# A written order for the late columns of a hybrid decoder layer, keys turned 256 rows at a time, and RWKV's propagators in one stretch

## The chip, the cores and the metric

The kernel runs on one core of a Trainium2 chip. The metric is the device time of one execution in microseconds; lower is better. The engines named below are PE (TensorE, matrix products and transposes), DVE (VectorE), ACT (ScalarE), POOL (GpSimd) and SP (SyncE, whose queue issues most DMAs).

## The reference

One inference step of one layer, for a prompt of 1024 tokens and eight decode samples. Everything reads the same normalised input `h`:

```python
h = rms_norm(x, ln_g)
q, kv, gates, z_nsa, u, z_rw, q_mem, z_mem = split_in(h @ w_in)
o_nsa = ...   # 8 heads: compressed blocks, top-16 selected blocks and a window of 512, mixed by gates
# RWKV-7, 4 heads of 64, per token:
sa = einsum('bhvk,bhk->bhv', s, -kk_t)
s  = s * w_t + sa * b_t + v_t * k_t
y_t = einsum('bhvk,bhk->bhv', s, r_t)
# memory: 256 rows
mkv = rms_norm(mem, g) @ w_kv        # keys get their own norm
o_mem = softmax(norm(q_mem) @ k.T * SCALE) @ v
cat = concat([o_nsa * silu(z_nsa), norm(y) * silu(z_rw), o_mem * silu(z_mem)])
y = x + cat @ w_out
```

The compressed keys come from an MLP over 32 rows at stride 16 (`compress`). The outputs also hold the new key and value rows, the final RWKV state and the memory's keys and values.

## The kernel before

All is 32-bit. A product of full precision is made of three fast ones: each operand is split into a high part (ACT copies it to the fast format, `whi`) and a low part (DVE subtracts, `wlo`), and high times high, high times low and low times high are summed in PSUM.

The work has three phases. In phase 1 the input projection is done in 21 *columns*, blocks of 128 output columns of `w_in`, in the order of the table `ORDER`. A column is done for two halves of the tokens. Its products are named `p_pr`, 24 per 512 tokens: 24 of 512 columns in one half, and 24 of 256 with 24 of 264 in the other, where the last 8 are the samples. Its result is drained by ACT and DVE (`zt` for the gate columns, `nr_o` and the like for queries and keys) and stored by SP to a scratch in memory (`z_d`, `q_d`, `k_d`, `v_d`).

The recurrence of RWKV is done in four quarters Q of the tokens in the matrix form of the delta rule (`rwkv_prep`, `rwkv_state`). It is a chain of small products on PE with evacuations on DVE and ACT between them, so `drive` puts column products between its steps as fill: a step yields the microseconds of PE work that should stand behind it. The order on PE is there written by the code: `InOrder` ties every PE instruction to the one before it, and keeps a running sum of PE time, `clock`. At the end of a quarter, `rwkv_state` forms `p_x` (the corrected rows, drained to `W` by ACT and `UV` by DVE), the propagators `p_g` (drained to `PT` and `GT`), the rows `p_yy`, and four rounds of `p_z<-Zn,PT`, each drained to `Zn`. `rwkv_out` normalises the result and stores it (`y_d<-y_c`). `rwkv_close` turns the final state with two transposes, also named `p_s`, as are the scores of the attention later.

When the fill is used up (17 columns, `EARLY`), the tail of Q = 3 and what follows are on a plain PE: the scheduler of the framework chooses the order by its own costs and priorities. There `ahead` interleaves, eight instructions to one step (`BG`):

- the last four columns (17 to 20), by `self.columns(cols[EARLY:])`, drawn in groups of 8;
- `attn_keys`, eight tiles of 128 key rows: each is loaded twice (two DMAs in 256 B pieces, so that each head stands on both halves of the partitions, `kd`), turned by four transposes (`p_k`) and split into `kh` and `kl`;
- `prompt_cmp` (the compressed keys: turned rows `p_xt`, the products `p_hid`, then `p_co`, whose normalised result is turned by a last `p_k` and drained to `ckh`, `ckl`);
- `mem_kv` (the memory's rows `mx` turned by `p_mT`, split into `mhi` and `mlo`, and 48 products `p_mo` in blocks of two of the eight k tiles), and `q_stack(7)` (the first queries, `p_q`).

Phase 2 is the attention, and begins with the scores `p_s<-kh,qs`; phase 3 is the output projection. PSUM tiles that are used for turning come from one pool of two buffers (tag `tr`); `p_g`, `p_yy`, `p_z` and `p_mo` use another (tag `w`).

```python
            for _ in group(late, 8):
                for _ in islice(bg, BG):
                    pass
```

Of the kernel before, what the change touches and what calls it, by code (L numbers as in the profile page):

```python
# [10 lines left out]
F32 = mybir.dt.float32  # L11
# [15 lines left out]
KB = 2  # L27
FREE = 0
ORDER = [4, 1, 11, 2, 3, 6, 5, 7, 13, 17, 10, 15, 0, 9, 8, 14, 12, 18, 16, 19, 20]
EARLY = 17  # L30
BG = 8
# [82 lines left out]
class Step:  # L114
# [356 lines left out]
    def phase1(self):  # L471
# [8 lines left out]
        with ExitStack() as ctx:  # L480
# [91 lines left out]
            self.pe = nc.tensor  # L572
# [10 lines left out]
            for _ in bg:  # L583
                pass

    def ahead(self):

        def keys():
            for i in range(8):
                self.attn_keys(i)  # L590
                yield
            yield from self.q_stack(7)

        self.mem_x()
        yield from weave(chain(self.prompt_cmp(), self.mem_kv()), keys())
# [232 lines left out]
    def rwkv_state(self, Q):  # L828
# [103 lines left out]
        GT, PT = [None] * 2, [None] * 2  # L932
        half = [slice(p * 64, p * 64 + 64) for p in range(2)]
        for t in range(2):
            GT[t] = self.rs.tile([128, 2, 2, 64], F32, name="GT", tag=f"GT{t}")
            PT[t] = self.rs.tile([128, 2, 2, 64], F32, name="PT", tag=f"PT{t}")
            pgs = [self.pw.tile([128, 4, 64], F32, name="p_g", tag="w") for _ in range(2)]
            for k in range(2):
                for c in range(2):
                    for h in range(2):  # L940
                        for pg, o, p in zip(pgs, half, range(2)):
                            x = AM[o, 2 * p + t, 2 * c + h, 64:128] if k else bkT[t][o, c, p, h * 64:h * 64 + 64]
                            PE.matmul(pg[half[h], 2 * k + c, :], W[t][o, 2 * c + h, :], x, start=True, stop=True)
            for p, pg in enumerate(pgs):
                V.tensor_tensor(PT[t][:, :, p, :], pg[:, 0:2], bc(self.eye2[:, None, :], [128, 2, 64]), op=OP.add)
            for p, pg in enumerate(pgs):
                V.tensor_tensor(GT[t][:, :, p, :], pg[:, 2:4], ar[:, :, t, 1, p, :], op=OP.add)
            if t == 0:
                yield 0.9
# [6 lines left out]
        yield 0.9  # L956
# [8 lines left out]
        for n in range(4):  # L965
            Zn = self.rc.tile([128, 2, 64], F32, name="Zn", tag="Z", bufs=5)
            for c in range(2):
                for h in range(2):
                    PE.matmul(pz[half[h], n, c, :], PT[n // 2][half[h], c, n % 2, :], Zs[n][half[h], c, :],
                              start=False, stop=True, skip_group_check=True)  # L970
            V.tensor_tensor(Zn[:], pz[:, n], bc(self.gC[:, :, n:n + 1], [128, 2, 64]), op=OP.mult)
            Zs.append(Zn)
            if n < 3:
                yield 0.8
        self.Z = Zs[4]
        for t in range(2):
            for c in range(2):
                for p, h in ((0, 0), (1, 1), (1, 0), (0, 1)):
                    PE.matmul(pyy[h][half[1 - p], t, c, :], GT[t][half[h], c, p, :], Zs[2 * t + p][half[h], c, :],
                              start=False, stop=(c == 1), skip_group_check=True)  # L980
# [32 lines left out]
    def rwkv_close(self):  # L1013
        nc, O = self.nc, self.O
        ps = self.pw.tile([128, 2, 128], F32, name="p_s", tag="w")
        for c in range(2):
            nc.tensor.transpose(ps[:64, c, :], self.Z[:, c, :], self.ident[:])
# [15 lines left out]
    def cmp_consts(self):  # L1033

        nc, I = self.nc, self.I
        V, PE = nc.vector, nc.tensor
# [45 lines left out]
    def compress(self, xt, n, hid):  # L1082

        nc = self.nc
        V, A, PE = nc.vector, nc.scalar, self.te
        V.memset(hid[:, :, 63:64], 0.0)
        for e in range(2):
            ps = self.pM.tile([128, n, 64], F32, name="p_hid", tag="m")
            for m in range(8):
                PE.matmul(ps[:], self.w1s[e][:, m].rearrange("p a b -> p (a b)"), xt(e, m), start=(m == 0), stop=(m == 7))  # L1090
            hs = self.wk.tile([64, n, 63], F32, name="c_hs", tag="c_hs", bufs=2)
            A.activation(hs[:], ps[64:, :, 1:], AF.Copy)
            V.tensor_tensor(hs[:], hs[:], ps[:64, :, :63], op=OP.add)
# [4 lines left out]
            yield  # L1098

    def cmp_out(self, hid2):  # L1100
# [3 lines left out]
        nc.tensor.matmul(ps[:, :128], hid2, self.w2d[:].rearrange("p a b -> p (a b)"), start=True, stop=True)  # L1104
# [20 lines left out]
    def mem_kv(self):  # L1125
        nc, I, O = self.nc, self.I, self.O
        V, A, PE = nc.vector, nc.scalar, nc.tensor
        xs = self.mem_rows
        his = [self.slot(j, [128, 4, 256], F32R, f"mhi{j}") for j in (4, 0)]
        los = [self.slot(j, [128, 4, 256], F32R, f"mlo{j}") for j in (5, 1)]  # L1130
        for k in range(8):
            ps = self.pM.tile([128, 512], F32, name="p_mT", tag="m")
            for t in range(2):
                PE.transpose(ps[:, t * 128:(t + 1) * 128], xs[t][:, k * 128:(k + 1) * 128], self.ident[:])
            g = self.v("mem_norm_g", k)
            hi, lo = his[k // 4][:, k % 4, :], los[k // 4][:, k % 4, :]
            A.activation(hi, ps[:, :256], AF.Copy, scale=g)
            V.scalar_tensor_tensor(lo, ps[:, :256], g, hi.bitcast(F32), op0=OP.mult, op1=OP.subtract)
            yield
        po = [self.pw.tile([128, 512], F32, name="p_mo", tag="w") for t in range(2)]  # L1140
        for k in range(0, 8, 2):
            raw = self.wr.tile([128, 2, 512], F32, name="wraw")
            nc.sync.dma_start(raw[:], I["w_mem_kv"][0, k * 128:(k + 2) * 128, :].rearrange("(k p) c -> p k c", p=128))
            wh = self.wp.tile([128, 2, 512], F32R, name="whi")
            wl = self.wp.tile([128, 2, 512], F32R, name="wlo")
            A.activation(wh[:], raw[:], AF.Copy)
            V.tensor_tensor(wl[:], raw[:], wh[:].bitcast(F32), op=OP.subtract)
            yield
            for j in range(2):
                for t in range(2):  # L1150
                    cs = slice(t * 128, (t + 1) * 128)
                    h, l = his[k // 4][:, (k + j) % 4, cs], los[k // 4][:, (k + j) % 4, cs]
                    for i, (a, w) in enumerate(((h, wh), (h, wl), (l, wh))):
                        PE.matmul(po[t][:], a, w[:, j], start=(k + j == 0 and i == 0), stop=(k + j == 7 and i == 2))
            yield
        dst = O["mem_kv_prompt"]
        for t in range(2):
# [5 lines left out]
            yield  # L1163
# [67 lines left out]
    def attn_keys(self, i, tag="m"):  # L1231
        nc = self.nc
        A, G = nc.scalar, nc.gpsimd
        kk = self.kt.tile([128, 4, 2, 64], F32, name="kd4", tag="kd4", bufs=KB)
        for s in range(2):
            nc.sync.dma_start(kk[:, :, s, :], self.k_d[i * 128:(i + 1) * 128, :].rearrange("t (j d) -> t j d", d=64))
        if i % 4 == 0:
            nc.sync.dma_start(self.vs[i // 4][:].rearrange("p k b g d -> p k (b g d)"),
                              self.v_d[i * 128:(i + 4) * 128, :].rearrange("(k p) c -> p k c", p=128))
        ps = self.pM.tile([128, 4, 128], F32, name="p_k4", tag=tag)  # L1240
        for j in range(4):
            nc.tensor.transpose(ps[:, j, :], kk[:, j].rearrange("p s d -> p (s d)"), self.ident[:])
        kh, kl = (x[i // 4][:, :, i % 4 * 128:i % 4 * 128 + 128] for x in (self.kh, self.kl))
        A.activation(kh, ps[:], AF.Copy)
        nc.vector.tensor_tensor(kl, ps[:], kh.bitcast(F32), op=OP.subtract)

    def prompt_cmp(self):
        nc, I, O = self.nc, self.I, self.O
        V, A, G, PE = nc.vector, nc.scalar, nc.gpsimd, nc.tensor
# [11 lines left out]
        for e in range(2):  # L1261
# [4 lines left out]
            xs.append(x)  # L1266
        yield from self.cmp_consts()
# [15 lines left out]
        yield  # L1283
# [1232 lines left out]
```

## Time and profile before

| | us |
|---|---|
| median of three runs | 937.47 (934.78 to 939.75) |
| profiled execution | 936.7, of which the span 934.9 |
| PE busy | 899.3 (96%) |
| DVE, ACT, POOL busy | 648.0, 434.2, 178.7 |
| granted clock of PE, mean | 0.998 |

The span runs from the first to the last instruction that the profile shows. The stretch of the change is the last quarter's tail (from 409 us on), the late columns (to 497 us), and, for the propagators, a few microseconds in each of the three quarters before. A row of a timeline gives the start, the length, the engine, the line of the code, the operation and its tiles, the shape, the number of instructions and, in brackets, the idle time ahead with what ended it. The ends of products on PE are modelled, so the time from one start to the next tells better how fast they follow each other.

### The profile page before, as it was taken

To read this page: it belongs to the slowest core of one execution; us is meant where nothing else is said; L and a number is where in the kernel's file an instruction comes from. 1 tells how busy PE (TensorE), PEld (TensorE's weight loads), DVE (VectorE), ACT (ScalarE), POOL (GpSimd) and SP (SyncE) were. 2 spreads that over 40 slices of the span, in tenths; PEclk is the share of its full clock that TensorE was granted. 3 is DMA by queue.
4 is the path that set the end of the run, shared out by engine and by line. 5 is a ranking of instruction groups with operands and counts; after the bars stand their busy time and mean duration, and the time that the engine had idled before them with its cause. 6 is when DMAs were issued, how large, how long until landed. Compare 5 with 4: busy or idle time off the path is not lost.

```text
span 934.9 us, 24813 instructions
## 1 busy us (share of the span) xinstructions
PE 899.3 (96%) x9911; PEld 762.7 (82%) x9911; DVE 648.0 (69%) x2013; ACT 434.2 (46%) x987; POOL 178.7 (19%) x270
## 2 busy tenths in 40 slices
PE   8999999999999999999899999999999999999998
PEld 7998888877878788778777788888887887887976
DVE  7668679864777559946457866765678996548454
ACT  7654324232443234213446666666566766424211
POOL 2000000000000000000104444544344765112010
PEclk9999999999999999999999999999999999999999
DMA  8521313241321205524429313432130036986561
GB/s 278 130 78 35 104 41 105 61 115 48 84 86 52 77 19 143 136 65 132 138 85 275 99 56 108 132 108 60 32 87 10 10 113 168 330 249 218 179 239 47
DMA packets 134698, 105.96 MB, mean 113 GB/s; under 512 B 34641, under 2 KB 120600, under 8 KB 134456
## 3 DMA queue, kind: packets, MB, share of 16 engines
q1 hardware_dynamic: 129592, 92.64, 33.8%
q0 software_dynamic: 3200, 10.49, 3.2%
q8 instruction: 78, 1.28, 0.5%
q10 hardware_dynamic: 1792, 1.26, 0.5%
q14 instruction: 36, 0.29, 0.1%
HBM read 85.77 MB, written 22.78 MB: 116 GB/s over the span
## 4 chain that ended last, share of the span: by engine, by line
PE 73%; DVE 17%; ACT 5%; DMA 2%; issue 2%; POOL 0%; SPq 0%; DVEq 0%; ACTq 0%
PE p_pr L86 20%; PE p_out L86 9%; PE p_pr L306 5%; PE p_o L86 5%; PE p_s L86 5%; PE p_pT L86 5%; PE p_hid L86 3%; ACT p L1416 2%; DVE p L1409 2%; PE p_it L86 1%; PE p_iy L86 1%; PE p_sc L86 1%; DVE pt L1377 1%; DVE wlo L283 1%; PE p_tk L86 1%
## 5 line engine op out<-in xcount | busy, mean ns | idle before, releaser
L86 PE MATMUL p_pr<-h,whi 128*128 128x512 f32 (+2 forms) x976 | 237.0, 336 | 2.0 <-DVE zt L318 2.0
L86 PEld LDWEIGHTS p_pr<-h,whi 128*128 128x128 f32 x976 | 158.6, 189 | 19.5 <-issue 2.4
L86 PE MATMUL p_pr<-h,wlo 128*128 128x512 f32 (+2 forms) x488 | 157.6, 326 | 0.6 <-DVE wlo L283 0.6
L1447 POOL TENSOR_SCALAR p<-p,fac,gates 128x640 f32<-128x640 f32 (+7 forms) x128 | 103.3, 817 | 110.9 <-DVE fac L1443 71.1
L1416 ACT ACTIVATE p<-p,nm 128x640 f32<-128x640 f32 (+7 forms) x128 | 93.1, 728 | 56.3 <-DVE nm L1409 51.3
L86 PEld LDWEIGHTS p_pr<-h,wlo 128*128 128x128 f32 x488 | 91.4, 189 | 9.3 <-DVE wlo L283 0.8
L86 PE MATMUL p_pT<-ident,p 128*128 128x128 f32 x528 | 70.8, 279 | 6.9 <-POOL p L1447 1.9
L1075 POOL MEMSET w2d<- 128x128 f32 x1 | 0.2, 204 | 377.2 <-PE p_iy L86 377.2
L86 PEld LDWEIGHTS p_pT<-ident,p 128*128 128x128 f32 x528 | 56.8, 140 | 18.1 <-issue 6.6
L1409 DVE CUSTOM_DVE_ANT_0 p<-p_s,bmask 128x512 f32<-128x512 f32 (+7 forms) x96 | 60.3, 659 | 16.1 <-PE p_s L86 15.4
L306 PE MATMUL p_pr<-h,whi 128*128 128x264 f32 (+2 forms) x320 | 69.3, 310 | 0.0
L86 PE MATMUL p_o<-pt,vs 128*64 128x128 f32 x1056 | 67.9, 276 | 0.4 <-DVE cat L1485 0.4
L283 DVE TENSOR_TENSOR wlo<-wraw,whi 128x1024 fp32r<-128x1024 f32 x33 | 40.3, 1221 | 36.9 <-ACT whi L282 32.6
L86 PE MATMUL p_s<-kh,qs 128*128 128x512 f32 (+3 forms) x191 | 65.2, 354 | 0.2 <-DVE nm L1409 0.2
L282 ACT ACTIVATE whi<-wraw 128x1024 fp32r<-128x1024 f32 x34 | 36.0, 1059 | 59.6 <-PE p_pr L86 47.1
L86 PEld LDWEIGHTS p_o<-pt,vs 128*64 128x64 f32 x1056 | 57.0, 137 | 7.5 <-issue 3.9
L86 PE MATMUL p_s<-kl,qs 128*128 128x512 f32 (+3 forms) x192 | 60.3, 334 | 0.0
L1377 DVE COPY pt<-p_pT 128x512 f32<-128x512 f32 (+1 forms) x72 | 48.2, 673 | 13.2 <-PE p_pT L86 12.4
L306 PEld LDWEIGHTS p_pr<-h,whi 128*128 128x128 f32 x320 | 51.5, 188 | 3.1 <-issue 0.2
L86 PE MATMUL p_out<-woh,chi 128*128 128x512 f32 x128 | 51.7, 404 | 0.0
L86 PE MATMUL p_out<-woh,clo 128*128 128x512 f32 x128 | 50.2, 392 | 0.4 <-DVE clo L2352 0.4
L86 PE MATMUL p_out<-wol,chi 128*128 128x512 f32 x128 | 49.9, 390 | 0.0
(551 smaller groups left out, 1884.3 us busy)
## 6 DMA issues: line engine op xcount, KB each, us to landing
wraw<-in_w_in_dram SPq DMA_DIRECT2D x34, 512.0 KB
pg<-in_c_pool_dram SPq DMA_DIRECT2D x32, 256.0 KB
pg<-in_c_pool_dram SPq DMA_DIRECT2D x48, 128.0 KB
x<-in_x_prompt_dram SPq DMA_DIRECT2D x8, 512.0 KB
z_d<-zt SPq DMA_DIRECT2D x16, 256.0 KB
cat<-z_d SPq DMA_DIRECT2D x8, 512.0 KB
xres<-in_x_prompt_dram POOLq DMA_DIRECT2D x16, 256.0 KB, 3.8
out_dram<-xres POOLq DMA_DIRECT2D x16, 256.0 KB, 3.0
```

The source lines that it names most:

```text
L86: self.last = getattr(self.engine, op)(*a, **k)
L282: nc.scalar.activation(hi[:, :, :n], raw[:, :, :n], AF.Copy)
L283: (low or nc.vector).tensor_tensor(lo[:, :, :n], raw[:, :, :n], hi[:, :, :n].bitcast(F32), op=OP.subtract)
L306: self.last_mm = self.pe.matmul(ps[:m, :b - a], w[:, k, :m], h[k][:, a:b], start=(k == 0 and i == 0), stop=(k == 7 and i == 2))
L1075: nc.gpsimd.memset(w2d[:], 0.0)
L1377: nc.vector.tensor_copy(pt[:, :n], ps[:, :n])
L1409: return V.tensor_tensor_reduce(halves(x), halves(ps), m, -1.0, 3.0e38, op0=OP.add, op1=OP.min, accum_out=nm[:, h, b:b + 1])
L1416: e = A.activation(x, x, AF.Exp, scale=-1.0, bias=nm[:, h, b:b + 1], accum_out=sm[:, h, b:b + 1])
L1447: nc.gpsimd.tensor_scalar(x, x, f[:, h, b:b + 1], gate[:, hd + h, 1 + b:2 + b], op0=OP.mult, op1=OP.mult)
```

## The change

Three things change.

1. The late columns have an order written by the code. After the columns of the fill, `self.pe` and a new `self.te` are an `InOrder`, so every transpose and product of this stage is tied to the one ahead. `mix` draws column products until 1.4 us of PE clock (`LAG`) have passed, and then lets each of two streams take a step when it is ready, that is, when the clock has passed the microseconds that its last step yielded. The streams are `keys_ahead` and `cmp_ahead`. The memory's work is split: `mem_turn` turns and splits the rows at the end of `cmp_ahead`, two k tiles to a PSUM tile, and `mem_product` does the 48 products between columns 19 and 20; it first runs what is left of `cmp_ahead`.
2. Keys are loaded 256 rows at a time and once (`load_keys`, four DMAs of 256 KB in 1 KB pieces, `KB` = 3 buffers), turned with 16 transposes in place of 32, split on 64 partitions at a time, and copied to the other 64 partitions by eight DMAs on SP (`copy_keys`).
3. `rwkv_state` forms all 64 `p_g` at once, with one tile each for `PT` and `GT`, drained by four additions of 128x256 instead of eight of 128x128. It yields 1.6 once in place of 0.9 twice.

```diff
-            self.pe = nc.tensor
+            self.pe = self.te = InOrder(tc, nc.tensor, self.pe.last)
             self.rwkv_close()
...
-            bg = self.ahead()
-            late = self.columns(cols[EARLY:])
-            for _ in group(late, 8):
-                for _ in islice(bg, BG):
-                    pass
+            work = [self.keys_ahead(), self.cmp_ahead()]
+            self.mix(work, chain(self.columns(cols[EARLY:-1]), self.mem_product(work[1]), self.columns(cols[-1:])))
...
+    def keys_ahead(self):
+        rows = [self.load_keys(n) for n in range(3)]
+        yield 4.0
+        for n in range(4):
+            self.turn_keys(n, rows[n])
+            if n == 0:
+                rows.append(self.load_keys(3))
+            yield 2.8
+            if n % 2:
+                self.copy_keys(n // 2)
+                self.load_values(n // 2)
+        yield from self.q_stack(7)
...
+    def mix(self, work, fill):
+        te = self.te
+        ready = {g: te.clock for g in work}
+        while work or fill:
+            for g in list(work):
+                if te.clock >= ready[g] or not fill:
+                    us = next(g, -1)
+                    if us == -1:
+                        work.remove(g)
+                    ready[g] = te.clock + (us or 1.5)
+            start = te.clock
+            while fill and te.clock < start + LAG:
+                if next(fill, None) is None:
+                    fill = None
...
-            if t == 0:
-                yield 0.9
...
-        yield 0.9
+        yield 1.6
...
-        for k in range(8):
-            ps = self.pM.tile([128, 512], F32, name="p_mT", tag="m")
+        for k0 in range(0, 8, 2):
+            ps = self.pM.tile([128, 2, 256], F32, name="p_mT", tag="m")
...
+    def load_keys(self, n):
+        kk = self.kt.tile([128, 2, 2, 128], F32, name="kd4", tag="kd4", bufs=KB)
+        self.nc.sync.dma_start(kk[:].rearrange("p i j d -> p i (j d)"),
+                               self.k_d[n * 256:(n + 1) * 256, :].rearrange("(i p) c -> p i c", p=128))
+        return kk
+    def copy_keys(self, h):
+        for x in (self.kh[h], self.kl[h]):
+            for g in range(2):
+                o, to = slice(g * 64, g * 64 + 64), slice(64 - g * 64, 128 - g * 64)
+                self.nc.sync.dma_start(x[to, g::2].bitcast(F32), x[o, g::2].bitcast(F32))
```

How the instructions move is shown at four places; lines are those of each kernel's own code.

The first is PE at the end of quarter 3. Before, from the second round of `Zn` to the transposes of the state:

```order
L306 MATMUL p_pr<-h_7_260,whi 128x256
L86 MATMUL p_z<-Zn,PT 64x64 x4
L306 MATMUL p_pr<-h_7_259,wlo 128x256
L306 MATMUL p_pr<-h_0_245,whi 128x264
L306 MATMUL p_pr<-h_0_246,whi 128x264
L306 MATMUL p_pr<-h_0_245,wlo 128x264
L86 MATMUL p_z<-Zn,PT 64x64 x4
L86 MATMUL p_yy<-Zn,GT 64x64 x16
L1017 MATMUL p_s<-ident,Zn 64x128 x2
```

After, from the corrected rows on:

```order
L86 MATMUL p_x<-R,Ti 64x128 x16
L86 MATMUL p_g<-bkT,W 64x64 x16
L86 MATMUL p_g<-AM,W 64x64 x16
L86 MATMUL p_z<-UV,bkT 64x64 x16
L86 MATMUL p_yy<-UV,AM 64x64 x16
L86 MATMUL p_z<-Zn,PT 64x64 x16
L86 MATMUL p_yy<-Zn,GT 64x64 x16
L86 MATMUL p_s<-ident,Zn 64x128 x2
L86 MATMUL p_pr<-h_0_245,whi 128x256
```

The 27 column products that stood among and just ahead of these steps now stand behind them.

The second is SP's queue at the first key load. Before:

```order
L1021 DMA out_dram<-S_out 64x64 x4
L319 DMA z_d<-zt 128x512
L321 DMA z_d<-zt 128x8
L1011 DMA y_d<-y_c 128x256 x2
L1236 DMA kd_6401<-k_d 128x4x64 x2
L1238 DMA vs_6259<-v_d 128x4x256
L1236 DMA kd_6437<-k_d 128x4x64 x2
```

After:

```order
L1039 DMA out_dram<-S_out 64x64 x4
L1029 DMA y_d<-y_c 128x256 x2
L1265 DMA kd_6242<-k_d 128x2x256
L1265 DMA kd_6244<-k_d 128x2x256
L1265 DMA kd_6246<-k_d 128x2x256
L1292 DMA vs_6227<-v_d 128x4x256
```

The key loads have become fewer and larger; the stores of `y_c` stand ahead of them in both.

The third is PE at the first key tile. Before, the first `p_k` is 75 column products behind the state's transposes, and these are the last of them:

```order
L306 MATMUL p_pr<-h_0_246,whi 128x264
L306 MATMUL p_pr<-h_0_245,wlo 128x264
L306 MATMUL p_pr<-h_1_247,whi 128x264
L306 MATMUL p_pr<-h_1_248,whi 128x264
L306 MATMUL p_pr<-h_1_247,wlo 128x264
L1242 MATMUL p_k_6405<-ident,kd_6401 128x128 x4
```

After:

```order
L86 MATMUL p_pr<-h_3_251,whi 128x264
L86 MATMUL p_pr<-h_3_252,whi 128x264
L86 MATMUL p_pr<-h_3_251,wlo 128x264
L86 MATMUL p_k_6350<-ident,kd_6242 128x128 x4
L86 MATMUL p_pe<-ident,pe_rows 128x32
L86 MATMUL p_pr<-h_4_253,whi 128x264
```

The names `h_k_...` are the input's tile k and its part: after, the first `p_k` stands in the middle of the first half of column 17, behind 36 products.

The fourth is PE at the turned memory rows. Before:

```order
L1190 MATMUL p_k<-ident,kd 128x128
L1134 MATMUL p_mT<-ident,mx_6337 128x128
L1134 MATMUL p_mT<-ident,mx_6356 128x128
L306 MATMUL p_pr<-h_2_810,wlo 128x512
L306 MATMUL p_pr<-h_3_813,whi 128x512
L306 MATMUL p_pr<-h_3_814,whi 128x512
L1134 MATMUL p_mT<-ident,mx_6337 128x128
L1134 MATMUL p_mT<-ident,mx_6356 128x128
L1154 MATMUL p_mo<-whi,mhi_6750 128x512
```

After, the 16 `p_mT` follow the last product of column 19 and that `p_k` without a break; this is where they end:

```order
L86 MATMUL p_mT<-ident,mx_6248 128x128
L86 MATMUL p_mT<-ident,mx_6267 128x128
L86 MATMUL p_mo<-whi,mhi_6811 128x512
L86 MATMUL p_mo<-wlo,mhi_6811 128x512
L86 MATMUL p_mo<-whi,mlo_6813 128x512
```

The transposes, two at a time between products before, are now all ahead of the products. One move is on DVE: the split `wlo` for column 17, which stood ahead of the inverse's chain (`iT`) in quarter 3, stands some 40 rows later, behind the second `iY`.

More of the change, by code (lines that the diff above doesn't have):

```diff
@@ L26 @@
 PTB = 8
-KB = 2
+KB = 3
 FREE = 0
@@ L577, in phase1, with cmp_ahead @@
             self.pM = Tag(self.ptr, "tr")
-            bg = self.ahead()
-            late = self.columns(cols[EARLY:])
-            for _ in group(late, 8):
-                for _ in islice(bg, BG):
-                    pass
[L583 to L592, printed above, removed]
-        self.mem_x()
-        yield from weave(chain(self.prompt_cmp(), self.mem_kv()), keys())
+            self.mem_turned = False
+            work = [self.keys_ahead(), self.cmp_ahead()]
[12 more added lines that the diff above has]
+        yield from self.q_stack(7)
+    def cmp_ahead(self):
+        self.mem_x()
+        yield from self.prompt_cmp()
+        yield from self.mem_turn()
+        self.mem_turned = True
+    def mix(self, work, fill):
[12 more added lines that the diff above has]
+                    fill = None
     def drive(self, work, fill):
@@ L931, in rwkv_state @@
         yield 0.6
-        GT, PT = [None] * 2, [None] * 2
         half = [slice(p * 64, p * 64 + 64) for p in range(2)]
[L934 to L938, printed above, removed]
+        GT = self.rs.tile([128, 2, 2, 2, 64], F32, name="GT", tag="GT")
+        PT = self.rs.tile([128, 2, 2, 2, 64], F32, name="PT", tag="PT")
+        pgs = [self.pw.tile([128, 2, 4, 64], F32, name="p_g", tag="w") for _ in range(2)]
+        for k in range(2):
+            for t in range(2):
                 for c in range(2):
@@ L942, in rwkv_state @@
                             x = AM[o, 2 * p + t, 2 * c + h, 64:128] if k else bkT[t][o, c, p, h * 64:h * 64 + 64]
[L943 to L947, printed above, removed]
-            if t == 0:
-                yield 0.9
+                            PE.matmul(pg[half[h], t, 2 * k + c, :], W[t][o, 2 * c + h, :], x, start=True, stop=True)
+        for p, pg in enumerate(pgs):
+            V.tensor_tensor(PT[:, :, :, p, :], pg[:, :, 0:2], bc(self.eye2[:, None, None, :], [128, 2, 2, 64]), op=OP.add)
+        for p, pg in enumerate(pgs):
+            V.tensor_tensor(GT[:, :, :, p, :], pg[:, :, 2:4], ar[:, :, :, 1, p, :].rearrange("p c t e -> p t c e"), op=OP.add)
         pz = self.pw.tile([128, 4, 2, 64], F32, name="p_z", tag="w")
@@ L968, in rwkv_state @@
                 for h in range(2):
-                    PE.matmul(pz[half[h], n, c, :], PT[n // 2][half[h], c, n % 2, :], Zs[n][half[h], c, :],
+                    PE.matmul(pz[half[h], n, c, :], PT[half[h], n // 2, c, n % 2, :], Zs[n][half[h], c, :],
                               start=False, stop=True, skip_group_check=True)
@@ new lines, in mem_block @@
+    def mem_block(self, k):
+        nc, I = self.nc, self.I
+        raw = self.wr.tile([128, 2, 512], F32, name="wraw")
+        nc.sync.dma_start(raw[:], I["w_mem_kv"][0, k * 128:(k + 2) * 128, :].rearrange("(k p) c -> p k c", p=128))
+        wh = self.wp.tile([128, 2, 512], F32R, name="whi")
+        wl = self.wp.tile([128, 2, 512], F32R, name="wlo")
+        nc.scalar.activation(wh[:], raw[:], AF.Copy)
+        nc.vector.tensor_tensor(wl[:], raw[:], wh[:].bitcast(F32), op=OP.subtract)
+        return wh, wl
@@ L1140, in mem_kv, with mem_product @@
+    def mem_product(self, turns):
+        nc, O = self.nc, self.O
+        A, PE = nc.scalar, self.te
+        while not self.mem_turned:
+            next(turns, None)
+        his, los = self.mem_hi, self.mem_lo
         po = [self.pw.tile([128, 512], F32, name="p_mo", tag="w") for t in range(2)]
+        w = self.mem_block(0)
         for k in range(0, 8, 2):
-            raw = self.wr.tile([128, 2, 512], F32, name="wraw")
-            nc.sync.dma_start(raw[:], I["w_mem_kv"][0, k * 128:(k + 2) * 128, :].rearrange("(k p) c -> p k c", p=128))
@@ L1144, in mem_kv @@
[L1144 to L1148, printed above, removed]
+            (wh, wl), w = w, self.mem_block(k + 2) if k < 6 else None
             for j in range(2):
@@ L1152, in mem_kv @@
                     h, l = his[k // 4][:, (k + j) % 4, cs], los[k // 4][:, (k + j) % 4, cs]
-                    for i, (a, w) in enumerate(((h, wh), (h, wl), (l, wh))):
-                        PE.matmul(po[t][:], a, w[:, j], start=(k + j == 0 and i == 0), stop=(k + j == 7 and i == 2))
-            yield
+                    for i, (a, b) in enumerate(((h, wh), (h, wl), (l, wh))):
+                        PE.matmul(po[t][:], a, b[:, j], start=(k + j == 0 and i == 0), stop=(k + j == 7 and i == 2))
+                    yield STEP
         dst = O["mem_kv_prompt"]
@@ L1229, in slot @@
         return self.catp.tile(shape, dtype, name=name, tag=f"c{j}")
-    def attn_keys(self, i, tag="m"):
-        nc = self.nc
[L1233 to L1245, printed above, removed]
+    def load_keys(self, n):
[3 more added lines that the diff above has]
+        return kk
@@ new lines, in turn_keys @@
+    def turn_keys(self, n, kk):
+        nc = self.nc
+        ps = self.pM.tile([128, 2, 2, 128], F32, name="p_k4", tag="m")
+        for j in range(2):
+            for i in range(2):
+                self.te.transpose(ps[:, j, i, :], kk[:, i, j], self.ident[:])
+        c = slice(n % 2 * 256, n % 2 * 256 + 256)
+        for g in range(2):
+            o = slice(g * 64, g * 64 + 64)
+            x = ps[o].rearrange("p j i t -> p j (i t)")
+            kh, kl = self.kh[n // 2][o, g::2, c], self.kl[n // 2][o, g::2, c]
+            nc.scalar.activation(kh, x, AF.Copy)
+            nc.vector.tensor_tensor(kl, x, kh.bitcast(F32), op=OP.subtract)
@@ new lines, in copy_keys, with load_values @@
+    def copy_keys(self, h):
+        for x in (self.kh[h], self.kl[h]):
+            for g in range(2):
+                o, to = slice(g * 64, g * 64 + 64), slice(64 - g * 64, 128 - g * 64)
+                self.nc.sync.dma_start(x[to, g::2].bitcast(F32), x[o, g::2].bitcast(F32))
+    def load_values(self, h):
+        self.nc.sync.dma_start(self.vs[h][:].rearrange("p k b g d -> p k (b g d)"),
+                               self.v_d[h * 512:(h + 1) * 512, :].rearrange("(k p) c -> p k c", p=128))
```

42 lines of the change are left out of this document (22 added, 20 removed).

## The prediction

> **What bounds the kernel.** I read the busy table first.
>
> ```profile
> span 934.9 us, 24813 instructions
> PE 899.3 (96%) x9911; PEld 762.7 (82%) x9911; DVE 648.0 (69%) x2013; ACT 434.2 (46%) x987; POOL 178.7 (19%) x270
> ```
>
> PE is busy 899.3 of 934.9 us. All its idle time is 35.6 us, so the change can gain little by filling holes, and what it costs is counted in new holes. Next I read who keeps PE waiting in the stretch that the change rewrites (405 to 505 us), and PE's busy time from the first key product to the attention.
>
> ```profile
> PE p_k L1242 <- DMA kd<-k_d: 2.4, 2, 1.9
> PE p_mo L1154 <- DVE wlo L1147: 0.5, 1, 0.5
> PE p_k L1190 <- POOL kd L1183: 0.5, 1, 0.5
> PE p_pr L306 <- DVE wlo L283: 0.4, 2, 0.2
> ```
> ```profile
> 433.80:497.40 63.60, 59.45 (x383) 48.99 (x384) 31.44 (x102) 25.61 (x54) 3.19 (x6) 1.00 0.48 136
> ```
>
> The columns of the first rows are total, number and longest wait. The last row is a table of windows: 63.60 us long, PE busy 59.45 in 383 instructions, so 4.15 us of holes. The chain of waits through this place, with the two SP rows that stand in it:
>
> ```profile
> 421.49 0.75 DVE gn_s L998 x2
> ...
> 429.04 0.44 DVE y_c L1009
> 429.91 0.59 SPq L1236
> 430.55 3.17 DMA kd<-k_d
> 433.85 0.63 PE p_k L1242 x4
> ```
> ```profile
> 427.85 1.97 SPq L1011 DMA_DIRECT2D y_d<-y_c  x2
> 429.91 1.26 SPq L1236 DMA_DIRECT2D kd<-k_d  x2
> ```
>
> SP's queue goes in order. The two stores of `y_c` stand ahead of the first key load and wait for the last group norm, which DVE finishes 8 us after it began. So the keys are asked for at 429.91 and used at 433.85. PE did not notice: the scheduler had put 75 products `p_pr` there.
>
> **The change part by part.** *The tail of the recurrence* (propagators in one stretch, and no `p_pr` among its steps). The rows of before:
>
> ```profile
> 409.20 1.96 PE L86 MATMUL p_x<-R,Ti 64*64 64x128 f32 x32
> 410.76 1.75 DVE L930 COPY UV<-p_x 64x256 f32<-64x256 f32 x4 [0.82 <-ACT W L927]
> 412.53 0.49 DVE L945 TENSOR_TENSOR PT<-p_g,c_rw 128x128 f32<-128x128 f32 x2
> 415.61 1.19 PE L86 MATMUL p_yy<-UV,AM 128*64 128x64 f32 x32
> 416.74 0.45 PE L86 MATMUL p_z<-Zn,PT 64*64 64x64 f32 x8
> 417.23 0.29 DVE L971 TENSOR_TENSOR Zn<-p_z,gC 128x128 f32<-128x128 f32 x1 [1.61 <-PE p_z L86]
> 420.95 0.49 PE L306 MATMUL p_pr<-h,whi 128*128 128x264 f32 x2
> ```
> ```profile
> 414.08 0.62 PE p_g L86 x30
> ...
> 479.61 3.81 DMA wraw<-in_w_in_dram
> ```
>
> From `p_x` to the first `p_pr` behind `p_s` is 11.75 us, and it holds 23 `p_pr` of 0.118 us, 2.7 us of work; 9.05 us are its own. By the order of after nothing fills it. I walk it: `UV` is ready 3.3 us after `p_x`; 64 `p_g` at 0.62 for 30, then `p_z`, reach 4.3; the four wider adds of `PT` and `GT` (0.44 each, as `y_c` in the chain, of the same 128x256) hold back `p_yy`, which takes their PSUM, so `p_z<-Zn` begins near 6.6; four rounds of product, `Zn` and product take 0.85 each without fill (0.49 to `Zn`, 0.29 in it, a little to return). That ends at 10.4, so **+1.35** (0.5 to 2.5). In the three earlier quarters fill stands between these steps, behind both versions; I cost them at nothing, and their price without it would be the same 1.35 each.
>
> *A weight split moved.* Just before, DVE's split `wlo` stands ahead of the inverse's chain:
>
> ```profile
> 377.45 1.22 DVE L283 TENSOR_TENSOR wlo<-wraw,whi 128x1024 fp32r<-128x1024 f32 x1
> 383.38 0.74 PE L86 MATMUL p_iy<-iT,AM 32*32 32x32 f32 x64 [1.86 <-DVE rq_t L134]
> ```
>
> In after's DVE order it comes later and only one small step takes its place (I take 0.2): **-0.9** (-1.1 to 0; the memory rows' norm, now nearer, can eat it).
>
> *The key wait.* In after's PE order the first `p_k` stands behind 36 `p_pr` only (24 of 256 columns, 12 of 264). Their pitch, start to start:
>
> ```profile
> 424.66 0.63 PE L306 MATMUL p_pr<-h,whi 128*128 128x512 f32 x2
> 425.12 0.40 PE L306 MATMUL p_pr<-h,wlo 128*128 128x512 f32 x1
> ...
> 429.56 0.40 PE L306 MATMUL p_pr<-h,whi 128*128 128x256 f32 x2
> 429.79 0.28 PE L306 MATMUL p_pr<-h,wlo 128*128 128x256 f32 x1
> ```
>
> 0.23 each at 512, 0.117 at 256. So PE stands at `p_k` 4.3 us after `p_s`. The key load still stands behind `y_d` on SP, 8.96 us after `p_s` before (429.91 less 420.95); I take 8.7, since two DVE pieces leave the norm's chain. Then 3.6 to land: 3.8 from issue before for two loads of half the size, and 3.81 for the 512 KB of `wraw` in the last row above, so 3.6 for one of 256 KB. PE waits 12.3 - 4.3 = 8.0 us, against 0.6 before: **+7.4** (6.5 to 8). The whole of PE's order is behind this wait: `p_pr` is there in plenty, but after it.
>
> The rule on small pieces speaks for the change here: the Trainium skill, "DMA: Bandwidth & Descriptors", section Specifications, asks for 512 B or more per transfer, and before's keys go in 256 B pieces, now 1 KB. By its fixed 2 us and its 436 GB/s a landing of 2.6 us would be my estimate, the wait 1.0 less and the sum 944.0; no row of before shows this size.
>
> *The clock.* What a hole can cost, in windows before, at and behind PE's longest:
>
> ```profile
> 275.24 0.73 PE L86 MATMUL p_pr<-h,whi 128*128 128x512 f32 x2 [1.96 <-DVE zt L318]
> ```
> ```profile
> 273.00:276.40 3.40, 1.44 (x8) 1.04 (x7) 3.27 (x13) 0.39 (x1) 0.00 (x0) 1.00 0.25 81
> 276.40:279.90 3.50, 3.50 (x10) 2.71 (x9) 0.00 (x0) 0.00 (x0) 0.00 (x0) 0.51 0.40 148
> ```
>
> After 1.96 us idle the granted clock (column PEclk) was 0.51 for 3.5 us: half of that is lost, 1.7 us. The 1.9 us wait for keys had no such drop (1.00 in the row 433.80:497.40). An 8 us hole is four times as long: **+1.7** (0 to 3.4).
>
> *Holes that go.* Keys in four tiles, loaded early, and the written order remove the waits listed above after 433.85: at least the 4.15 us of holes, at most 6.4 counted start to start (ends are modelled, which hides some 0.15 per hole): **-6.0**. *Transposes:* 16 fewer, by
>
> ```profile
> 442.01 0.44 PE p_k L1242 x4
> ```
>
> 0.11 each: **-1.75**. The eight copies across partitions go on SP and finish long before the attention; their cover is the 30 us of columns behind them. If it failed, `p_s` would wait one landing, 3.2 us. The key splits become 8 pieces on ACT and 8 on DVE with the same elements; DVE's are hidden, except for the next term.
>
> *Holes that come.* (i) A piece of `kl` now stands on DVE behind column 19's `wlo`, and `p_xt` waits for its PSUM: one `wlo`, **+1.3** (0 to 1.5). (ii) The end of column 19, where all 16 transposes of memory stand in a row and `p_mo` behind them:
>
> ```profile
> L283 DVE TENSOR_TENSOR wlo<-wraw,whi 128x1024 fp32r<-128x1024 f32 x33 | 40.3, 1221 | 36.9 <-ACT whi L282 32.6
> L282 ACT ACTIVATE whi<-wraw 128x1024 fp32r<-128x1024 f32 x34 | 36.0, 1059 | 59.6 <-PE p_pr L86 47.1
> ```
> ```profile
> 431.76 0.68 DVE L318 SCALAR_TENSOR_TENSOR zt<-zt,p_pr 128x512 f32<-128x512 f32 x1
> ...
> 466.98 0.47 ACT L1137 ACTIVATE mhi<-p_mT,vec 128x256 fp32r<-128x256 f32 x1
> 467.49 0.48 DVE L1138 SCALAR_TENSOR_TENSOR mlo<-p_mT,vec,mhi 128x256 fp32r<-128x256 f32 x1 [0.21 <-ACT mhi L1137]
> ```
>
> From the column's end E: ACT splits memory's second block (1.06, it needed the column's buffer), DVE its low part (1.22), then the column's `zt` (0.68) and `ckl`, a quarter of it (I take 0.3): E+3.3. Only then `mlo`, and `mhi` and `mlo` of one PSUM tile alternate (0.47 and 0.48). Tile 4's transposes wait until tile 2 is drained, two pairs more: E+6.0, and `p_mo` starts at E+6.6 with 1.7 us of PE work in between: **+4.9** (2 to 6). Before, products stood between the transposes. (iii) Column 20's `wlo` stays late by **+0.3**.
>
> Sum: 1.35 - 0.9 + 7.4 + 1.7 - 6.0 - 1.75 + 1.3 + 4.9 + 0.3 = +8.3 us. The columns not done in the tail are only moved. The profiled execution took 936.7 us, 0.8 under the median 937.47 of the three runs; 936.7 + 8.3 = **945.0**. Behind `p_s` the attention has the same rows in the same order, so the delay is carried to the end.
>
> **The rivals.** *The key wait is hidden* (not slower): if the norm's chain ended early enough for the load to be asked for 0.7 us after `p_s` instead of 8.7, the wait and its clock would go: 945.0 - 7.4 - 1.7 = 935.9. Each microsecond that `y_d` is earlier takes one off. For it: ACT and DVE are freer, since `zt` and `peT` leave the chain (0.5 us). Against: its length is a chain of small DVE steps that nothing shortens. *The stall behind column 19 is covered*: if ACT and DVE, idle during the key wait, are so far ahead that memory's split and `zt` are done at E, (ii) falls to 1.5: 941.6, and with a quick landing 940. Against: the split needs the column's own buffer, so it can't start before E. *Two drops of the clock*: the second hole, 4.9 us in pieces, halves the clock as well and the first for longer: 945.0 + 1.7 + 1.7 = 948.4, to 951. The row 276.40 speaks for it, and the undropped 1.9 us wait against. The Trainium skill, "TensorE: Matmul & The Clock Gate", section "Part 1: The HAM clock gate", halves the clock after an idle window of about 3.4 us that runs freely; the first hole holds two such windows, the second none in one piece. The trace agrees with the 3.4 us length, but a hole of 1.96 us sufficed there.
>
> **How the numbers follow.** Forecast 0.54, key wait hidden 0.10, covered stall 0.18, two drops 0.13, anything else 0.05. The three lower cases spread by about 3 us each. The range from 935 to 951 leaves out half of the first rival and some of the rest, under 2 in 10; the forecast's own range is 942 to 948. The runs of before lie 0.5% apart, so 0.5%, 4.7 us, is about what can be told from no change: faster means below 932.8 and is the first rival's lower part and half of the rest, 0.07; same, up to 942.2, is its other part, the covered stall and the forecast's lower edge, 0.23; slower is 0.70.
>
> **What would show it.** The first `p_k` would show some 8 us of idle put down to the key load, with `y_d` issued just before it, and a granted clock under 1 in the next 3.5 us. `p_mT` and the first `p_mo` would show 4 to 5 us of idle behind `mlo`. The wait for a second `kd` would be gone, and no other wait in the stretch would be over 1.5 us. The attention would begin 8 us later. I am wrong if the key load is issued before PE's thirty-sixth `p_pr`, if `p_mo` follows the transposes within 2 us, or if the three earlier quarters lose time to the narrower fill.

## The result, and the profile after

The changed kernel takes 945.59 us (median of seven runs, 943.39 to 948.62), against 937.47 before (934.78 to 940.22): 1.0084 times as long, 95% interval 1.006 to 1.0109. The forecast was 945.0. The profiled execution of after took 946.61 us, 1.0 over its median; its span is 9.9 us longer than before's, and PE is busy 1.1 us less:

```profile
span 944.8 us, 24747 instructions
PE 898.2 (95%) x9895; PEld 765.5 (81%) x9895; DVE 647.0 (68%) x1997; ACT 434.2 (46%) x987; POOL 178.7 (19%) x270
```

So PE's idle time grew by 11.0 us, from 35.6 to 46.6. Products at a lower clock count as busy, so what the clock cost is hidden in the busy time. The waits of PE in after's rewritten stretch, 404 to 515 us, say who kept it waiting (total, number, longest):

```profile
PE p_k L86 <- DMA kd<-k_d: 7.4, 1, 7.4
PE p_pt L86 <- DVE kl L1282: 2.1, 1, 2.1
PE p_mT L86 <- DVE ckl L1223: 1.8, 1, 1.8
PE p_mT L86 <- DVE mlo L1158: 1.6, 2, 0.8
PE p_z L86 <- DVE Zn L989: 1.2, 3, 0.4
PE p_pr L86 <- DVE wlo L283: 0.6, 1, 0.6
```

The chain of waits at the first key tile reads as it did before, with one difference: now PE stands idle until it ends.

```profile
426.00 0.44 DVE y_c L1027
426.46 0.33 SPq L1029
426.84 2.95 DMA kd<-k_d
429.84 1.13 PE p_k L86 x4
...
431.91 8.46 DMA q<-q_d
440.42 0.41 issue
440.83 0.60 ACT kh L1281
```

The last three rows are a wait that I had not seen coming: ACT's queue held the split of the first queries (`qhl`, the 0.41 that the chain calls issue) ahead of a key split `kh`, and the query load, issued just behind the last keys and the values, took 8.46 us.

The clock of after, in windows around the three large holes (the first number is the window's length, the next PE's busy time; the granted clock is third from the right):

```profile
426.30:429.70 3.40, 0.00 (x0) 0.00 (x0) 0.60 (x4) 0.00 (x0) 0.00 (x0) 0.57 0.59 174
429.70:433.10 3.40, 3.26 (x14) 2.87 (x15) 1.02 (x3) 1.18 (x2) 0.00 (x0) 0.50 0.89 261
...
439.90:443.40 3.50, 1.42 (x9) 1.08 (x8) 1.30 (x5) 1.91 (x4) 1.46 (x2) 1.00 0.24 56
443.40:446.80 3.40, 3.40 (x17) 3.21 (x16) 2.63 (x5) 2.25 (x3) 0.00 (x0) 0.57 0.78 191
...
478.00:481.40 3.40, 1.29 (x8) 0.84 (x8) 2.32 (x6) 1.65 (x4) 0.00 (x0) 1.00 0.69 142
481.40:484.90 3.50, 3.17 (x10) 2.72 (x11) 2.02 (x5) 1.47 (x4) 0.00 (x0) 0.51 0.23 87
```

Each hole is followed by some 3.4 us of busy PE at about half the clock; the first is long enough for the drop to begin within it. That is three times 1.5 to 1.7 us in this execution.

### The profile page after: what moved, and what is told of

Read it like the earlier page. It is cut to its first block, busy times and chain, and to the rows that moved or that the text cites. A ratio compares the mean times of both kernels' runs of the same rounds, so it can differ in the third digit from the quotient of the medians.

```text
span 944.8 us, 24747 instructions
## 1 busy us (share of the span) xinstructions
PE 898.2 (95%) x9895; PEld 765.5 (81%) x9895; DVE 647.0 (68%) x1997; ACT 434.2 (46%) x987; POOL 178.7 (19%) x270
## 4 chain that ended last, share of the span: by engine, by line
PE 69%; DVE 18%; ACT 6%; DMA 3%; issue 3%; POOL 0%; SPq 0%; DVEq 0%; ACTq 0%
PE p_pr L86 23%; PE p_out L86 9%; PE p_o L86 5%; PE p_s L86 5%; PE p_pT L86 4%; PE p_hid L86 3%; ACT p L1465 3%; PE p_pr L306 2%; DVE p L1458 2%; DMA wraw<-in_w_in_dram 1%; PE p_sc L86 1%; DVE pt L1426 1%; PE p_it L86 1%; DVE wlo L283 1%; PE p_tk L86 1%
## 5 line engine op out<-in xcount | busy, mean ns | idle before, releaser
L86 PE MATMUL p_pr<-h,whi 128*128 128x512 f32 (+2 forms) x1168 | 282.7, 335 | 2.0 <-DVE zt L318 2.0
L86 PEld LDWEIGHTS p_pr<-h,whi 128*128 128x128 f32 x1168 | 191.5, 191 | 21.9 <-issue 2.6
L86 PE MATMUL p_pr<-h,wlo 128*128 128x512 f32 (+2 forms) x584 | 189.3, 327 | 1.2 <-DVE wlo L283 1.2
L86 PEld LDWEIGHTS p_pr<-h,wlo 128*128 128x128 f32 x584 | 110.7, 190 | 11.4 <-DVE wlo L283 1.6
L1426 DVE COPY pt<-p_pT 128x512 f32<-128x512 f32 (+1 forms) x72 | 48.2, 673 | 12.9 <-PE p_pT L86 12.1
L1424 ACT ACTIVATE pt<-p_pT 128x512 f32<-128x512 f32 (+1 forms) x72 | 41.3, 578 | 17.4 <-PE p_pT L86 16.6
L86 PEld LDWEIGHTS p_s<-kh,qs 128*128 128x128 f32 x191 | 36.1, 189 | 3.3 <-DVE nm L1458 0.8
```

The lines of the kernel that those rows point to most:

```text
L86: self.last = getattr(self.engine, op)(*a, **k)
L1424: nc.scalar.activation(pt[:, :n], ps[:, :n], AF.Copy)
L1426: nc.vector.tensor_copy(pt[:, :n], ps[:, :n])
```

## The experiments

All times below are medians; the kernel before ran beside each of them on the same chip (936.3 to 937.4), and the ratios are to it. The changed kernel stood at 1.0084, 8.1 us over the kernel before.

**Key loads on POOL's queue**, so that nothing stands ahead of them:

```diff
-        self.nc.sync.dma_start(kk[:].rearrange("p i j d -> p i (j d)"),
+        self.nc.gpsimd.dma_start(kk[:].rearrange("p i j d -> p i (j d)"),
```

> The changed kernel with one edit: the four key loads are issued by POOL's queue instead of SP's, so they no longer stand behind the two stores of y_c. PE's order is the same. Theory (the 7.4 us wait at the first p_k is only SP's order, and the hole halves the clock behind it): that wait falls under 1 us and the granted clock in the first products of the stretch is 1, so the time falls by 7.4 + 1.7 = 9 us against the changed kernel, to about 936.5. Rival (the work behind the keys is bound by ACT and DVE or the transfers, and the wait only moves to the next step): a fall of under 4 us, to 942 or more, with a longer wait at the second or third key tile.

939.53 us, ratio 1.0032 (1.0008 to 1.0055): 2.9 us over the kernel before, so some 5 us of the loss are gone, where the theory gave 9. The wait for the key load is gone from the list of PE's waits in the same stretch of this kernel, and so is the one at `p_pt`; these stand in their place:

```profile
PE p_pc L86 <- issue: 1.3, 1, 1.3
...
PE p_xt L86 <- issue: 1.1, 1, 1.1
PE p_k L86 <- DVE peT L1062: 1.0, 1, 1.0
```

`peT` is a small copy on DVE that stands behind the whole norm chain of `y_c`. So does the key split `kl`, whose end (428.75 and 0.69 in DVE's timeline) frees the PSUM for `p_pc` at 429.55. So DVE's queue is a second thing behind SP's, and gives 2.3 us back. The clock was not saved there either: both waits fall into one window, and the next is at half.

```profile
426.67:430.08 3.41, 1.18 (x21) 0.97 (x25) 2.72 (x9) 1.46 (x3) 0.00 (x0) 1.00 0.51 123
430.08:433.50 3.42, 3.42 (x29) 2.45 (x21) 1.27 (x4) 0.53 (x2) 0.05 (x1) 0.50 0.99 345
```

The time lies between the two theories: the hole was SP's order, but it hid waits for DVE that cost PE again, and half a window of clock with them.

**Memory's rows turned earlier**, ahead of `cmp_out`:

```diff
-        yield from self.mem_turn()
-        self.mem_turned = True
...
+        yield from self.mem_turn()
+        self.mem_turned = True
         ck, cv = self.cmp_out(hid[:].rearrange("p n c -> p (n c)"))
```

> The changed kernel with one edit: mem_turn runs before cmp_out, among the products of column 19, instead of at its end. Theory (the holes at the end of column 19 come from 16 transposes in a row on two PSUM buffers, behind ACT's and DVE's work for the column): the four waits of p_mT and p_k, 4.9 us in all, fall under 1.5 us and the half clock behind them goes, so 945.6 - 3.5 - 1.7 = about 940.5. Rival (the split of memory's second weight block, which needs the column's buffer, holds p_mo in any order): the wait turns up ahead of the second block of p_mo and the time falls by under 2 us, to 943.5 or more.

950.14 us, ratio 1.0156 (1.0126 to 1.0186): slower, which neither theory gave. The waits of `p_mT` did go (0.4 is left), but the compressed keys' chain came late, as this kernel's list of PE's waits shows:

```profile
PE p_k L86 <- POOL kd L1212: 3.4, 1, 3.4
PE p_co L86 <- issue: 2.3, 1, 2.3
```

The last step of turning was drawn by `mem_product`, which went on into `p_co`; the yield behind it was lost, and only 3 products stood between `p_co` and the `p_k` that needs its norm, a chain that took 5.5 us in the kernel before and takes as long here (479.87 to 485.32). The edit made its own hole, so it says nothing on the old one's cause.

**The queries' split behind the last key split on ACT:**

```diff
-            nc.scalar.activation(kh, x, AF.Copy)
+            self.last_kh = nc.scalar.activation(kh, x, AF.Copy)
...
-            with self.tc.issue_after(self.exp.ins) if i == 6 else ExitStack():
+            with self.tc.issue_after(self.exp.ins) if i == 6 else self.tc.issue_after(self.last_kh.ins) if first else ExitStack():
                 A.activation(hl[:, :, 0], q[:, 4 * b:4 * b + 4], AF.Copy)
```

> The changed kernel with one edit: on ACT the split of the first queries (qhl) stands behind the last kh, so ACT no longer waits for the query load (8.5 us after its issue) ahead of a key split. Theory: the 2.2 us wait of p_pt goes, and with it a stretch of 3.4 us at half the clock: 945.6 - 2.2 - 1.7 = about 941.7. Rival (the wait is DVE's kl or PSUM in any case, or the query work is late next): a fall of under 1 us, to 944.5 or more, with a new wait at p_q.

946.46 us (942.63 to 951.18), ratio 1.0124 (1.0086 to 1.0162): no gain that can be told. The wait at `p_pt` is gone from the profile, and the next one is in this kernel's list of PE's waits, at the place where the prediction had put it:

```profile
PE p_k L86 <- DMA kd<-k_d: 7.5, 1, 7.5
...
PE p_xt L86 <- issue: 1.1, 1, 1.1
```

DVE's timeline of this kernel has the cause that the prediction gave: column 19's `wlo` ahead of `kl`, whose PSUM `p_xt` (at 443.74) needs.

```profile
441.69 1.23 DVE L283 TENSOR_TENSOR wlo<-wraw,whi 128x1024 fp32r<-128x1024 f32 x1 [0.71 <-ACT whi L282]
442.94 0.69 DVE L1282 TENSOR_TENSOR kl<-p_k,kh 64x512 fp32r<-64x512 f32 x1
```

That saves 1 us of waiting and not 2.1. Its four runs spread by 8.5 us, and their mean granted clocks go with them: 942.63 at 0.993, 945.43 at 0.991, 947.50 at 0.987, 951.18 at 0.984.

**The three edits together:**

> The three edits of the other runs together. Theory (three separate holes, each with its own cause): the falls add up, 945.6 - 9 - 5 - 3.9 = about 928, below the kernel before (937.5). Rival (they share one cause, or each hole covers for the next): the sum of the single falls is not reached by 4 us or more, about 933 or above.

943.01 us, ratio 1.0061 (1.0028 to 1.0094). The sum of the theory is far off, and must be: the second edit loses by itself.

**Memory's product behind column 20:**

```diff
-            self.mix(work, chain(self.columns(cols[EARLY:-1]), self.mem_product(work[1]), self.columns(cols[-1:])))
+            self.mix(work, chain(self.columns(cols[EARLY:]), self.mem_product(work[1])))
```

> The changed kernel with one edit: memory's product stands behind column 20 instead of ahead of it, so the transposes of memory's rows fall among column 20's products at their own pace. Theory (the 4.9 us at the end of column 19 come from turning in a row with nothing between): the waits of p_k and p_mT fall under 1.5 us in sum and the stretch at half the clock behind them goes, 945.6 - 3.5 - 1.7 = about 940.5, unless memory's keys come too late for the attention, which would show as PE waiting there. Rival (the waits follow the transposes wherever they stand, as they did when turned earlier): 944 or more.

945.87 us, ratio 1.0094 (1.0067 to 1.0122): no gain. The waits of `p_mT` are gone from the list, as the theory had it, and this one has come into this kernel's list, taken to 530 us:

```profile
PE p_s L86 <- DVE nm L1458: 3.6, 2, 3.2
```

It is the attention's first softmax (`nm`), in DVE's queue behind the norm of memory's keys, which can only begin when the last `p_mo` is done. The saved time is given back some 25 us later.

**The propagators alone**, in the kernel before (only `rwkv_state` as in the diff):

> The kernel before with the third part of the change alone (propagators in one stretch). Theory: the three earlier quarters gain the 1.2 us that the changed kernel shows there at the third p_x, and the tail of the last quarter loses under 1: within 1.5 us of the kernel before, 935.5 to 937. Rival (the third part is what makes the tail dear, 1.35 us by my working, and the earlier gain is a different count of clock windows): 938 or more.

937.13 us, ratio 1.0004 (0.9987 to 1.0021): no effect that can be told. Of the 1.2 us that after's profile shows at the third `p_x` (323.05 against 324.24), 0.7 is the clock's: before's stretch at half, from 276 on, lies wholly ahead of its third `p_x`, and after's, from 321 on, only in part. Some 0.4 may be the edit's: from the first `p_x` to the second it is 91.2 us in the profiles with it (after's and this one's) and 91.6 in before's.

**The hole filled** with 60 transposes whose result is not read:

```diff
+        ps = self.pM.tile([128, 4, 128], F32, name="p_fill", tag="m")
+        for n in range(60):
+            self.te._do("transpose", ps[:, n % 4, :], self.ident[:], self.ident[:])
         for n in range(4):
             self.turn_keys(n, rows[n])
```

> The changed kernel with 60 idle transposes of the identity on PE (0.11 us each, 6.6 us) in the hole ahead of the first key product; their result is not read, and the wait itself stays. Theory (the hole lets the clock fall, and the first 3.4 us behind it run at half): the first p_k starts where it did, within 0.5 us of 12.1 us behind the state's transposes, the granted clock behind it is 1, and the time falls by 1.7 us, to about 944. Rival (the half clock has nothing to do with the hole): it stays at half there, and the time is the same or later.

947.63 us (942.34 to 949.43), ratio 1.0101 (1.0063 to 1.014). The first `p_k` starts 12.15 us behind the state's transposes, as without the fill (12.12), and behind it this kernel's windows show the clock whole:

```profile
427.70:431.10 3.40, 2.62 (x24) 2.38 (x22) 0.56 (x4) 0.00 (x0) 0.00 (x0) 1.00 0.64 184
431.10:434.50 3.40, 3.29 (x22) 2.90 (x23) 1.51 (x3) 1.58 (x3) 0.00 (x0) 1.00 0.97 287
```

So in this execution the half clock goes with the hole. The time did not fall: PE came sooner to the instructions that wait for the query load on ACT, and stood 3.2 us at `p_xt` where it had stood 2.1 at `p_pt`, and this execution had stretches at half elsewhere (two from 479 on, two from 714 on). Four runs between 942.34 (clock 0.995) and 949.43 (0.989) can't tell 1.7 us.

**Four edits**: POOL's queue, a first yield of 9.0 in `keys_ahead`, the queries' split behind the keys, memory's product behind column 20.

> The changed kernel with four edits: key loads on POOL's queue, the first key tile turned 5 us of PE work later (a first yield of 9 instead of 4), the first queries' split behind the last kh, and memory's product behind column 20. Theory (each hole has its own cause and none is needed): PE's waits in the stretch fall from 20 us of start-to-start excess to under 9, and the clock has two stretches at half fewer, so 945.6 - 11 - 3.4 = about 931, faster than the kernel before (936.7 in these runs). Rival (holes move to the next step, as with memory turned early): 937 or above.

935.80 us, ratio 1.0006 (0.9983 to 1.003): the whole loss is recovered, but no more. That lies between the theory and the rival. The waits in front of the attention are down to `p_xt`'s 1.1 and the tail; in its first microseconds PE stands 3.2 us for the same `nm` as above, and DVE's timeline of this kernel (start, duration, engine, line, operation) shows what is ahead of it:

```profile
492.66 0.42 DVE L382 TENSOR_TENSOR mkv<-p_mo,rq_r 128x256 f32<-128x256 f32 x1
493.12 0.42 DVE L383 TENSOR_TENSOR mkv<-mkv,gains 128x256 f32<-128x256 f32 x1
...
494.26 1.22 DVE L1458 CUSTOM_DVE_ANT_0 p<-p_s,bmask 128x1024 f32<-128x1024 f32 x1
```

**The same with memory's product inside column 20**, its rows turned among the columns:

> As the kernel with the four better edits, but memory's rows are turned ahead of cmp_out, two k tiles at a time among the products of columns 19 and 20, and memory's product stands between the two halves of column 20. Theory (in the kernel with four edits PE stood 3.2 us at the attention's first scores, because DVE did the norm of memory's keys just there, and two stretches at half the clock followed): that hole goes, since the norm falls under column 20's second half; no hole over 1.5 us is left from the first key tile to the attention, and the time is 935.8 - 3.2 - 1.7 = about 931, 0.6% under the kernel before. Rival (the attention's start is bound by DVE and ACT anyway, so what is saved ahead of it is lost in it): 935 or above, with PE waiting for nm or pt there.

942.33 us, ratio 1.0052 (1.0028 to 1.0076): neither theory. `nm` is no longer waited for (0.2), but memory's weights are (PE's waits of this kernel):

```profile
PE p_mo L86 <- ACT whi L1171: 3.3, 3, 1.2
PE p_mo L86 <- DVE wlo L1172: 2.4, 3, 0.9
```

The pool of split weights has two buffers, and column 20's own weights keep one of them until its second half is done. So memory's blocks share the other, and each is split only when the last has been used: ACT's `whi` begins right behind the last `p_mo` of the block before, three times.

**The keys alone**, in the kernel before: `load_keys`, `turn_keys`, `copy_keys` as in the diff, with the scheduler's order:

> The kernel before with the second part of the change alone: keys loaded 256 rows at a time, turned with 16 transposes and copied across, in the scheduler's own order. Theory (the parts are not to blame, the written order is): 16 transposes fewer (1.75 us) and the wait for a later key load (1.9 us) gone, no 7 us hole at the first p_k, so 936.3 - 3 = about 933.5 (932 to 936). Rival (the new loading and copying is dear by itself, since ACT and DVE split keys in twice as many pieces that wait for each other): 939 or more.

933.85 us (930.62 to 938.59), ratio 0.9965 (0.9944 to 0.9986): a little faster than both kernels, as the theory had it. The key load is issued behind `y_d` here too, and PE hardly feels it in this kernel's list of waits:

```profile
PE p_k L1252 <- DMA kd<-k_d: 0.6, 1, 0.6
```

**Keys and propagators without the written order:**

> The kernel before with the second and third part of the change (keys 256 rows at a time, propagators in one stretch) and without the first: the scheduler chooses the order of the late columns. What the changed kernel has beyond this one is the written order and the split of memory's work. Theory (the written order is what costs): 0.3% to 0.5% under the kernel before, 932.5 to 934.5 where that stands at 937, so the order costs about 11 us. Rival (part of the loss comes with the propagators in the last quarter once keys are quick, or with both together): 937 or more.

933.81 us, ratio 0.9964 (0.9942 to 0.9987), as the theory had it. Its PE has the same number of instructions as the changed kernel's, and these waits of PE in the stretch:

```profile
PE p_mo L1159 <- DVE wlo L1152: 1.0, 2, 0.5
...
PE p_k L1249 <- DMA kd<-k_d: 0.4, 1, 0.4
```

What is left between this kernel and the changed one is the first part alone, the order with the split of memory's work that belongs to it: 1.0084 against 0.9964, 1.2% or some 11 us. That the first part costs, and the other two do not, is shown.

## Why the prediction was right, point by point

| step | forecast, us | shown |
|---|---|---|
| earlier quarters | 0 | 0 to -0.4; ratio 1.0004 with the propagators alone |
| tail, `p_x` to the first `p_pr` | +1.35 | 9.8 (408.07 to 417.88) against 9.05: +0.8 |
| weight split moved | -0.9 | about -0.5 (the wait at `p_iy` fell from 1.86 to 0.79, and a part was lost behind it) |
| wait for the first keys | +7.4 | 7.4 against 0.6 idle: +6.8 |
| half clock | +1.7 | some 5 in the profiled execution, some 4 by the clocks of all runs |
| (i) `kl` | +1.3 at `p_xt` | 2.1 at `p_pt`, another cause |
| (ii) end of column 19 | +4.9 | 5.0, start to start |
| (iii) column 20's `wlo` | +0.3 | 0.6 |

*The key wait* came as worked out: the load was asked for 8.7 us behind the state's transposes, and the keys were there after 12.1 (forecast 8.7 and 12.3). PE came to `p_k` after 4.7, where I had 4.3. The key load took 2.95 us in the chain, and 3.4 with its issue where I had taken 3.6. The Trainium skill, "DMA: Bandwidth & Descriptors", section "Anatomy of one DMA — SWDGE (gpsimd) path", has the fixed 2 us and the 436 GB/s behind my estimate of 2.6; it gives them for DMAs that POOL issues, these go by SP, and the measured one decides. That SP's order caused the wait is shown by the POOL run. The rival in which it is hidden was priced too low: some 5 us came back and not 9, since it left out that `peT` and `kl` stand on DVE behind the same chain as the stores, and that their waits halve the clock as well.

*The end of column 19* is right in size, and after's chain of waits goes step by step as worked out (the column's last product ends at 475.6; the issue row is DVE's split `wlo`):

```profile
475.63 1.07 ACT whi L1167
476.76 1.11 issue
477.87 0.68 DVE zt L318
478.54 0.20 DVE ckl L1223
478.75 0.40 DVE mlo L1158
...
481.73 1.09 PE p_mT L86 x4
482.82 3.78 PE p_mo L86 x12
```

The first `mlo` stands 3.1 us behind the column's end and the first `p_mo` 6.9 (forecast 3.3 and 6.6). With the product behind column 20 the waits went, which fits turning in a row; no run removed them at their place without making another.

*Step (i) failed in its mechanism.* I had `kl` wait for column 19's `wlo` on DVE. It waited for `kh` on ACT, which stood behind the first queries' split and so behind a DMA of 8.46 us. I had followed DVE's queue and not ACT's. With that wait removed, the one that I had named showed up behind `wlo`, 1.1 us at `p_xt`. So a sign of the forecast failed too: it had no further wait over 1.5 us in the stretch.

*The clock was sized for one hole.* In the profiled execution three holes were each followed by half clock, as in the rival with more drops. The runs bear it out: over the 71 executions of the kernel before that ran beside the experiments, the time falls by 8.2 us for each 0.01 of mean clock, and the changed kernel's median clock is 0.991 where theirs is 0.996. By that estimate the clock is some 4 us of the 8.1.

*So that the number is so near is in part luck.* The range held for the reasons given, with the key wait and the end of column 19 as its two large terms, but several terms missed and cancelled. Clock and (i) came out some 3 to 4 us dearer, the key wait, the tail and the earlier quarters about 1.5 cheaper, the weight split 0.4 dearer. Holes gone and transposes seem to be worth more than I took: from the first `p_k` to the attention the stretch grew by 14.4 us (62.8 to 77.2), of which 10.6 are the 66 products that the change leaves for it, and the terms as shown, with my -7.75 for holes and transposes, would have made it 15.5. No run tells these two apart. The rival with more drops stood at 948.4, and the slowest of after's seven runs took 948.62.

The attention began 10.4 us later (forecast 8) and the span ended 9.9 us later, so the delay was carried, as forecast.

## What to carry to other kernels

An order written out by hand turns every wait of one instruction into a wait of all that stand behind it, so each place in it needs the time at which its operand lands, and that includes what stands ahead of its DMA in the issuing queue and ahead of its evacuation on ACT and DVE; a sum of PE time knows none of these. Try the parts of a change apart: here the keys turned 256 rows at a time made the kernel 0.35% faster in the scheduler's order, and the written order hid that. When a hole is removed, look at once for who waits next, 2 us or 25 us on.

## What the runs showed of the hardware

A hole cost more than its length. In the traces the granted clock is whole or half, and it changes only at multiples of 3.41 us from its last change. Windows of after, cut at these places:

```profile
269.79:273.20 3.41, 2.50 (x21) 2.28 (x19) 3.41 (x19) 1.30 (x3) 0.00 (x0) 1.00 0.54 152
273.20:276.61 3.41, 2.35 (x10) 1.94 (x11) 2.09 (x7) 0.00 (x0) 0.00 (x0) 1.00 0.59 205
276.61:280.03 3.42, 3.42 (x19) 2.78 (x18) 1.50 (x3) 0.00 (x0) 0.00 (x0) 1.00 0.11 32
...
440.45:443.87 3.42, 1.57 (x8) 1.38 (x9) 1.62 (x6) 1.85 (x4) 1.46 (x2) 1.00 0.37 80
443.87:447.28 3.41, 3.41 (x17) 3.31 (x16) 2.76 (x5) 2.25 (x3) 0.00 (x0) 0.50 0.63 165
...
474.58:478.00 3.42, 1.97 (x11) 1.15 (x9) 2.26 (x10) 2.07 (x4) 0.41 (x2) 1.00 0.00 0
```

PE busy for 1.57 of 3.41 us was followed by half the clock, and so was the window from 478.00 with 1.29 (among the rows of the result), with no window idle as a whole; the one with 1.97 was not. From the run with the three edits, in the middle of the attention, a window with 2.21 that was:

```profile
707.60:711.00 3.40, 2.21 (x17) 1.69 (x16) 2.36 (x8) 3.04 (x8) 2.28 (x4) 1.00 0.00 0
711.00:714.40 3.40, 3.40 (x16) 3.02 (x15) 0.85 (x3) 0.06 (x1) 0.75 (x1) 0.55 0.02 5
714.40:717.80 3.40, 3.40 (x17) 2.56 (x18) 1.99 (x6) 1.57 (x5) 0.00 (x0) 0.50 0.00 0
```

So busy time alone does not decide. In the profiled executions here, from the first microseconds to the last, windows under 1.6 us busy were followed by half the clock every time, and windows between 1.6 and 2.3 sometimes; what decides among these stays open.

The Trainium skill, "TensorE: Matmul & The Clock Gate", section "Part 1: The HAM clock gate", says that the clock halves after an idle window of some 3.4 us and that the windows run freely. The length agrees. That a window must be idle does not: 1.29, 1.57 and 2.21 us busy of 3.4 were followed by half.

The same hole drops the clock in one execution and not in another. Before's wait of 1.96 us for `zt` lies in one window (1.44 us busy in the prediction's row) and is followed by half; after's wait for it, 1.97 us, is cut in two by the border at 273.20 and is not. That fits windows that run freely. Each stretch at half costs 1.7 us, and most of the spread of one kernel goes with the mean clock: the runs with the keys alone go from 930.62 us at a mean clock of 1.0 to 938.59 at 0.989. Differences under 2 us are not to be read from single executions here.
